# A two-layer hybrid trunk on one core: three sigmoids as Exp, Ln, Exp on ScalarE, and HGRN2's level products with two heads in the two halves of the array

## The chip, the cores and the metric

The kernel runs on one core of one Trainium2 chip. The metric is the device time in microseconds (us) of that core. Before the change the median of 3 runs is 2185.41 us (2184.63 to 2187.1).

## The reference, cut to what matters

Two layers over 512 tokens of width 1024 (256 context tokens and 256 latent tokens). Each layer normalizes, projects to a wide vector, runs three token mixers side by side (mLSTM, HGRN2, differential attention), projects back, and ends in a feed-forward block: a dense SwiGLU in layer 0, eight experts in layer 1. Everything is float32. The change touches HGRN2 and three gates:

```python
q = to_heads(jax.nn.silu(p['hg_q']), HG_H)            # silu(x) = x * sigmoid(x)
G = jnp.cumsum(g, axis=3)
a = jnp.einsum('bhntk,bhntsk,bhnsk->bhnts', q, decay, k)   # decay = exp(G_t - G_s), s <= t
o = jnp.einsum('bhnts,bhnse->bhnte', a, v) + ...           # both directions are added
jax.nn.sigmoid(p['ml_o']) * head_rms_norm(mlstm)           # 4 heads of 64
head_rms_norm(hgrn2) * jax.nn.silu(p['hg_g'])              # 4 heads of 64
```

HGRN2 has 4 heads with keys and values of width 64, so two heads fill the 128 partitions.

## The kernel before, in words

One function builds the program; a framework places each engine's instructions by its own estimate of when they are ready, so an instruction can stand ahead of one that was written earlier. Only stretches marked strict keep the written order, and none of the edits lies in one.

Products of float32 are made in two ways. Weights are split into a high part `whi` (ScalarE) and a low part `wlo` (VectorE), and three matmuls of the float32r type take the place of one (`mm3`). In HGRN2's levels the operands are plain float32, and the trace shows two weight loads and two matmuls for each product.

`mixer(l, X)` is one layer's mixer. `fm` is a generator that loads a megabyte of projection weights, multiplies 8 blocks for each 128 output columns into a bank `pp`, and hands the bank to a `use` function; `tm` does the same with tokens on the partitions. Generators wait in the list `work`, and `tick(n)` takes n steps out of it wherever the token mixers call it, so projection matmuls fill TensorE between the mixers' own. When `work` is empty, `tick` does nothing.

`use_hgq` (L752) turns the projected HGRN2 queries into silu: Exp on ScalarE, add 1 (L756) and reciprocal (L757) on VectorE, then the product. `use_o` (L993) does the same for the output gates of mLSTM and HGRN2, for four blocks of 128 columns a layer, each 128x512 in layer 0 and 128x256 in layer 1 (L998, L999). It is called late in the mixer, among the heads of the attention: `scores` and `values`, with softmax on ScalarE and VectorE. When the last `fm` is drained, `mix_t` transposes the mixers' output and multiplies it with the gates `og`.

`hgrn()` (L803) computes HGRN2 as a tree over token distance: distances 256 and 128 first (tiles `ez`), then for each pair of token tiles p0 seven levels with half widths h = 64, 32, 16, 8, 4, 2, 1, in a group of four and a group of three. Layer 0 has two pairs (14 levels), layer 1 one (7 levels). At the start of a group TensorE sums the logarithms of the gates into banks `pe` and ScalarE takes Exp into `el`. One level then is:

- VectorE, for each of two directions d: `el` times the keys in place (128x256), then the queries times `el` into a zero-padded tile `zq`. `zq` has room for two heads side by side; the head on partitions 0 to 63 fills its half of the columns, the other head the other half (L914 to L916: two instructions on 64 partitions), and the rest stays zero, set once by a memset on POOL (L801).
- TensorE: 8 products with all 128 rows and 128 moving columns, both heads in one product, because each head's rows meet zeros in the other head's columns. They go into two banks `pa`, one for each token tile i.
- `take` merges each bank into the result `at`: at the first level a copy on ScalarE, later a masked copy on VectorE (L890, 128x512), one for each token tile, so the first can start when half of the level's matmuls are done.
- then `tick(T_LEV)`: 4 steps of projections in layer 0, 3 in layer 1, as long as `work` lasts.

The diagonal after the last level (products `pa<-hq,hk`, masked copies at L938) already uses 64 rows for each head, and so do the products of `ez`.

Of the kernel before, what the change touches and what calls it, by code (L numbers as in the profile page):

```python
# [12 lines left out]
F32 = mybir.dt.float32  # L13
# [4 lines left out]
AF = mybir.ActivationFunctionType  # L18
ALU = mybir.AluOpType
AX = mybir.AxisListType  # L20

P = 128
# [87 lines left out]
def kernel(ctx: ExitStack, tc: tile.TileContext, t: dict, out: bass.AP):  # L110
    nc = tc.nc
# [3 lines left out]
    def ordered(op):  # L115
        def call(*args, **kw):
            ins = op(*args, **kw)  # L117
            if strict[0]:
                tc.keep_in_program_order(ins)
            return ins  # L120
        return call

    MM, TR = ordered(nc.tensor.matmul), ordered(nc.tensor.transpose)
    ACT = ordered(nc.scalar.activation)
    TT, TS = ordered(nc.vector.tensor_tensor), ordered(nc.vector.tensor_scalar)
# [12 lines left out]
    one = cp.tile([P, 1], F32, name="one")  # L138
# [10 lines left out]
    def bank(name, dt=F32):  # L149
        return psp.tile([P, 512], dt, tag="b", bufs=8, name=name)  # L150
# [374 lines left out]
    def mixer(l, X, banks=None):  # L525
# [16 lines left out]
        masks = mk.tile([P, 8, P], U8, name="masks")  # L542
# [16 lines left out]
        if l == 0:  # L559
            with tc.tile_pool(name=f"pn{l}", bufs=1) as pn:  # L560
# [56 lines left out]
                A, B, C = range(4), range(4, 6), range(6, 8)  # L617
# [30 lines left out]
        hg = hgp.enter_context(tc.tile_pool(name=f"hg{l}", bufs=1))  # L648
# [27 lines left out]
        def tm(ci, tiles, use):  # L676
# [3 lines left out]
            for n, g in enumerate(tiles):  # L680
# [11 lines left out]
                for i in g:  # L692
                    use(i, acc[i])


        hk = hx.tile([P, 2, 2, 512], F32, tag="b8a", name="hk")
        lh = hx.tile([P, 4, 4, P], F32R, tag="b8b", name="lh")
        ll = hx.tile([P, 4, 4, P], F32R, tag="b8c", name="ll")
        hq = hg.tile([P, 2, 512], F32, name="hq")
# [52 lines left out]
        def use_hgq(j, pp):  # L752
            e = hx.tile([P, 512], F32, tag="w2a", bufs=2, name="hq_e")
            a = slice(q0, 512)
            ACT(e[:, a], pp[:, a], AF.Exp, scale=-1.0)
            TS(e[:, a], e[:, a], scalar1=1.0, scalar2=None, op0=ALU.add)  # L756
            nc.vector.reciprocal(e[:, a], e[:, a])  # L757
            TT(hq[:, j, a], pp[:, a], e[:, a], op=ALU.mult)

        va = hg.tile([P, 4, 4, 65], F32, name="va")  # L760
# [35 lines left out]
                nc.vector.tensor_reduce(ss[:, 2 * n:2 * n + 2], sq, axis=AX.X, op=ALU.add)  # L796
            return ss

        zq = [hg.tile([P, 2, 2, P], F32, tag=f"zq{n}", name=f"zq{n}") for n in range(4)]
        for z0 in zq:  # L800
            nc.gpsimd.memset(z0, 0.0)  # L801

        def hgrn():  # L803
            opart = X[:, :, 256:512]
# [2 lines left out]
            for d in range(2):  # L807
                both = hx.tile([P, 2, 2, 512], F32, tag="w8", bufs=3, name=f"ez{d}")
                for li, lev in enumerate((256, 128)):
                    e = both[:, li]  # L810
# [20 lines left out]
                    for i0, i1 in (((0, 2), (2, 4)) if lev == 256 else tuple((i, i + 1) for i in range(lo // P, 4))):  # L831
                        key = i0 < 2 if lev == 256 else (i0 % 2 == 0) == (d == 0)
                        a = slice(i0 * P, i1 * P)
# [4 lines left out]
            half = [slice(0, 64), slice(64, 128)]  # L838
            for p0 in range(qt[0], 4, 2):
# [15 lines left out]
                if p0 == 2:  # L855
                    for s in range(2):
                        pa = [bank("pa") for _ in range(2)]
# [8 lines left out]
                pa = [bank("pa") for _ in range(2)]  # L866
# [8 lines left out]
                nc.vector.tensor_copy(opart[:, p0:p0 + 2, :], po.rearrange("p (i c) -> p i c", i=2))  # L875

            groups = (LEVELS[0:4], LEVELS[4:7])
            turn = 0  # L880
            for p0 in range(qt[0], 4, 2):
                pt_ = slice(p0 * P, p0 * P + 256)
                A = [hg.tile([P, 512], F32, tag="at", bufs=4, name="at") for _ in range(2)]

                def take(i, pa, n):
                    v = lambda a: a.rearrange("p (x t) -> p x t", x=4)
                    if n is None:
                        ACT(A[i], pa, AF.Copy)
                    else:
                        nc.vector.copy_predicated(v(A[i]), masks[:, n, :].unsqueeze(1).to_broadcast([P, 4, P]), v(pa))  # L890

                for gi, lv in enumerate(groups):
                    nl = len(lv)
                    z_ = []
                    for d in range(2):
                        e = hx.tile([P, 2, 4, 256], F32, tag="w8", bufs=3, name="el")
                        c0 = d * S_DIR + gi * 512
                        for c in range(2):
                            for i in range(2):
                                pe = bank("pe")  # L900
                                for part in (lh, ll):
                                    MM(pe[:, 0:nl * P], part[:, p0 + i, 2 * d + c, :], sums[:, c0:c0 + nl * P],
                                       start=(part is lh), stop=(part is ll))
                                ACT(e[:, c, 0:nl, i * P:(i + 1) * P], pe[:, 0:nl * P].rearrange("p (l t) -> p l t", l=nl), AF.Exp)
                        z_.append(e)
                    for n, h in enumerate(lv):
                        V = lambda a: a.rearrange("p c (n two h) -> p c n two h", two=2, h=h)
                        qs = []
                        for d in range(2):
                            ev = V(z_[d][:, :, n, :])  # L910
                            TT(ev[:, :, :, d, :], ev[:, :, :, d, :], V(hk[:, d, :, pt_])[:, :, :, d, :], op=ALU.mult)
                            q_ = zq[turn % len(zq)]
                            turn += 1
                            for par in range(2):  # L914
                                TT(q_[half[par], :, par, :].rearrange("p c (n h) -> p c n h", h=h), ev[half[par], :, :, 1 - d, :],
                                   V(hq[:, :, pt_])[half[par], :, :, 1 - d, :], op=ALU.mult)  # L916
                            qs.append(q_)
                        for i in range(2):
                            pa = bank("pa")
                            for c in range(2):  # L920
                                for d in range(2):
                                    MM(pa[:, c * 256:(c + 1) * 256].rearrange("p (a n two h) -> p a n two h", a=2, two=2, h=h)[:, :, :, 1 - d, :],
                                       z_[d][:, c, n, i * P:(i + 1) * P],
                                       qs[d][:, c, :, i * 64:(i + 1) * 64].rearrange("p a (n h) -> p a n h", h=h),
                                       start=True, stop=True, skip_group_check=True)
                            take(i, pa, None if gi + n == 0 else 4 * gi + n)
                        tick(T_LEV)
                pa = [bank("pa") for _ in range(2)]
                for i in range(2):
                    ia = slice((p0 + i) * P, (p0 + i + 1) * P)  # L930
                    for c in range(2):
                        for d in range(2):
                            for par in range(2):
                                at = i * 256 + c * P
                                MM(pa[par][:, at:at + P], hk[half[par], d, c, ia], hq[half[par], c, ia], start=(d == 0), stop=(d == 1))
                for par in range(2):
                    for i in range(2):
                        nc.vector.copy_predicated(A[i].rearrange("p (c a t) -> p c a t", c=2, a=2)[:, :, par, :],  # L938
                                                  masks[:, 7, :].unsqueeze(1).to_broadcast([P, 2, P]),
                                                  pa[par][:, i * 256:(i + 1) * 256].rearrange("p (c t) -> p c t", c=2))  # L940
                po = bank("po")
                for i in range(2):
                    for h in range(4):
                        MM(po[:, i * 256 + h * 64:i * 256 + (h + 1) * 64], A[i][:, h * P:(h + 1) * P], hv[:, p0 + i, h * 64:(h + 1) * 64],
                           start=(i + h == 0), stop=True, skip_group_check=True)
                o = opart[:, p0:p0 + 2, :]
                TT(o, po.rearrange("p (i c) -> p i c", i=2), o, op=ALU.add)
# [45 lines left out]
        def use_o(base):  # L993
            def use(j, pp):
                a = slice(q0, 512)
                o = og[:, base + j, a]
                ACT(o, pp[:, a], AF.Exp, scale=-1.0)
                TS(o, o, scalar1=1.0, scalar2=None, op0=ALU.add)  # L998
                nc.vector.reciprocal(o, o)  # L999
                w = vl + (V_MN, V_HN)[base // 2] + j  # L1000
                if base == 0:
                    TS(o, o, scalar1=sv[:, w:w + 1], scalar2=None, op0=ALU.mult)
                else:
                    STT(o, o, sv[:, w:w + 1], pp[:, a], op0=ALU.mult, op1=ALU.mult)
            return use
# [76 lines left out]
        for h in range(4):  # L1082
            if h % 2 == 0:

                S = [hx.tile([P, 4, 512], F32, tag=tg, name="S") for tg in ("b8b", "b8c")]
                for s in range(4):
                    a, b = st_rng[s]
# [8 lines left out]
            for d in range(2):  # L1096
# [10 lines left out]
                for s in range(4):  # L1107
                    W = hx.tile([P, 512], F32, tag="w2a", bufs=2, name="W")
                    bias = bT[:, s, row:row + 1]
# [14 lines left out]
                    for a, b in rng:  # L1124
                        for tt in range(a // P, b // P):
                            MM(num[d][:, tt, :], W[:, tt * P:(tt + 1) * P], va[:, s, h, :],
                               start=not started[d], stop=False, skip_group_check=True)
                            started[d] = True
            tr = slice(qt[0], 4)
            for d in range(2):  # L1130
# [7 lines left out]
                dst = hs_[:, tr, h * 64:(h + 1) * 64]  # L1138
# [47 lines left out]
        op = ow.enter_context(tc.tile_pool(name=f"ow{l}", bufs=1))  # L1186
# [120 lines left out]
        qs = {qt[0]: queries(qt[0])}  # L1307
        heads = [(tt, h) for tt in qt for h in range(4)]
        GATED = 8 if need else 6
        for n in range(len(heads) + 7):  # L1310
            if n < len(heads):
                tt, h = heads[n]
# [29 lines left out]
        with tc.tile_pool(name=f"xw{l}", bufs=1) as xw, tc.tile_pool(name=f"xo{l}", bufs=1) as xo:  # L1342
# [27 lines left out]
            two, three = steps  # L1370
# [591 lines left out]
```

## Time and profile before

| what | value |
| --- | --- |
| median of 3 runs | 2185.41 us |
| the profiled execution's own time | 2181.0 us |
| its span from first to last instruction | 2179.2 us |
| instructions in it | 27390 |
| mean granted TensorE clock | 0.985 of 2.4 GHz |
| PE / PEld busy | 2085.3 / 1672.8 us |
| VectorE (DVE) / ScalarE (ACT) busy | 1644.6 / 1249.3 us |
| POOL busy | 35.3 us |

PE is TensorE's matmul, PEld its weight load, which overlaps PE. The profile also gives windows (busy time of each engine in a stretch, the granted clock and the DMA share), the timeline (instructions in order of time, runs of equal ones merged: start, duration, engine, line, operation, how often, and in brackets the idle time before it with what ended it) and lists by tile. A helper issues most instructions, so most carry its line, L117, and are told apart by their tiles. In a merged row of n weight loads the last one starts one load's duration, 0.19 us, ahead of the row's end, so the distance between two starts is (duration - 0.19) / (n - 1).

### The profile page before, as it was taken

How to read it: one execution, taken by the hardware profiler on the slowest of the kernel's cores; microseconds unless marked ns; L12 is line 12 of the kernel's file. 1: busy time of each engine (PE TensorE's matmuls, PEld its weight loads, DVE VectorE, ACT ScalarE, POOL GpSimd, SP SyncE). 2: the span in 40 equal slices, each digit the busy share in tenths (PEclk: the TensorE clock that was granted, in tenths of full speed). 3: DMA queues.
4: the chain of work that ended last, by engine and by line, in shares of the span. 5: the costliest groups of instructions: out<-in, count | busy, mean ns of one | idle time of the engine just before them, and what ended most of it. 6: DMA issues, size and time to landing. Idle time of an engine off the chain costs nothing.

```text
span 2179.2 us, 27390 instructions
## 1 busy us (share of the span) xinstructions
PE 2085.3 (96%) x10326; PEld 1672.8 (77%) x10326; DVE 1644.6 (75%) x2324; ACT 1249.3 (57%) x1837; POOL 35.3 (2%) x47
## 2 busy tenths in 40 slices
PE   7998998999999999999879999999999999999997
PEld 4877776788788788887668888777778777777775
DVE  4758459769872347665879998888888888798987
ACT  3632455651222336534668776767777676767765
POOL 1000000010000001000000000000000000000000
PEclk9999999999999999999999999999999999999999
DMA  7430522238791331311258998899998999899992
GB/s 293 151 117 30 88 102 73 89 133 286 288 325 20 135 108 51 128 49 49 78 200 347 370 361 330 329 353 356 348 349 322 357 356 346 320 354 359 345 358 87
DMA packets 84301, 497.86 MB, mean 228 GB/s; under 512 B 19904, under 2 KB 20928, under 8 KB 26560
## 3 DMA queue, kind: packets, MB, share of 16 engines
q1 hardware_dynamic: 84160, 496.03, 61.8%
q8 instruction: 83, 1.36, 0.3%
q14 instruction: 58, 0.48, 0.1%
HBM read 493.86 MB, written 2.14 MB: 228 GB/s over the span
## 4 chain that ended last, share of the span: by engine, by line
PE 73%; DVE 16%; DMA 4%; ACT 4%; issue 3%; POOL 0%; SPq 0%; DVEq 0%; ACTq 0%; POOLq 0%
PE pg L117 20%; PE py L117 12%; PE pgu L117 10%; DVE wlo L117 9%; PE pp L117 8%; PE pd L117 5%; PE pr L117 4%; DMA raw<-w_eu 3%; PE st L117 3%; PE pa L117 2%; ACT whi L117 2%; PE po L117 1%; PE num L117 1%; PE pm L117 1%; DVE zq L117 1%
## 5 line engine op out<-in xcount | busy, mean ns | idle before, releaser
L117 DVE TENSOR_TENSOR wlo<-raw,whi 128x1024 fp32r<-128x1024 f32 x819 | 961.0, 1221 | 152.7 <-ACT whi L117 142.8
L117 ACT ACTIVATE whi<-raw 128x1024 fp32r<-128x1024 f32 (+1 forms) x820 | 813.2, 1055 | 187.3 <-PE pgu L117 75.6
L117 PE MATMUL pg<-wlo,TH 128*128 128x512 f32 x896 | 363.6, 406 | 5.8 <-DVE wlo L117 2.0
L117 PE MATMUL pg<-whi,TH 128*128 128x512 f32 x896 | 355.4, 397 | 0.0
L117 PE MATMUL pg<-whi,TL 128*128 128x512 f32 x896 | 352.1, 393 | 0.0
L117 PE MATMUL py<-whi,hhl 128*128 128x512 f32 x896 | 289.2, 394 | 0.0
L117 PEld LDWEIGHTS pg<-wlo,TH 128*128 128x128 f32 x896 | 168.3, 188 | 64.7 <-DVE wlo L117 31.3
L117 PEld LDWEIGHTS py<-whi,hhl 128*128 128x128 f32 x896 | 168.3, 188 | 39.4
L117 PEld LDWEIGHTS pg<-whi,TH 128*128 128x128 f32 x896 | 168.3, 188 | 39.3
L117 PEld LDWEIGHTS pg<-whi,TL 128*128 128x128 f32 x896 | 168.5, 188 | 35.1
L117 PE MATMUL py<-wlo,hhl 128*128 128x512 f32 x448 | 177.6, 396 | 1.0 <-DVE wlo L117 0.8
L117 ACT ACTIVATE hhl<-ph 128x512 fp32r<-128x512 f32 x56 | 33.4, 596 | 174.0 <-PE ph L1728 174.0
L117 PE MATMUL pgu<-TH,whi 128*128 128x512 f32 x320 | 127.2, 398 | 2.7 <-ACT whi L117 2.7
L117 PE MATMUL pgu<-TH,wlo 128*128 128x512 f32 x320 | 127.3, 398 | 0.2 <-DVE wlo L117 0.2
L117 PE MATMUL pgu<-TL,whi 128*128 128x512 f32 x320 | 127.0, 397 | 0.0
L117 PE MATMUL pp<-TH,whi 128*128 128x512 f32 (+1 forms) x304 | 117.9, 388 | 0.0
L117 PE MATMUL pp<-TH,wlo 128*128 128x512 f32 (+1 forms) x304 | 110.8, 365 | 0.4 <-DVE wlo L117 0.4
L117 PE MATMUL pp<-TL,whi 128*128 128x512 f32 (+1 forms) x304 | 111.1, 366 | 0.0
L274 DVE CUSTOM_DVE_ANT_0 junk<-raw,srow,sv 128x1024 bf16<-128x1024 f32 x80 | 102.5, 1282 | 3.4 <-DMA srow<-gd 2.0
L117 PEld LDWEIGHTS py<-wlo,hhl 128*128 128x128 f32 x448 | 84.1, 188 | 21.6 <-DVE wlo L117 2.7
L117 DVE TENSOR_TENSOR hhl<-ph,hhl 128x512 fp32r<-128x512 f32 x56 | 38.6, 690 | 55.4 <-ACT hhl L117 55.3
L117 PEld LDWEIGHTS pgu<-TH,whi 128*128 128x128 f32 x320 | 60.5, 189 | 17.6 <-ACT whi L117 3.2
(341 smaller groups left out, 3146.7 us busy)
## 6 DMA issues: line engine op xcount, KB each, us to landing
raw<-w_eg SPq DMA_DIRECT2D x112, 1024.0 KB, 6.3
raw<-w_eu SPq DMA_DIRECT2D x111, 1024.0 KB, 6.2
raw<-w_ed SPq DMA_DIRECT2D x111, 1024.0 KB, 6.5
raw<-w_mv SPq DMA_DIRECT2D x28, 1024.0 KB, 7.3
raw<-w_fm SPq DMA_DIRECT2D x22, 1024.0 KB, 4.9
raw<-w_fg SPq DMA_DIRECT2D x11, 1024.0 KB, 7.0
raw<-w_fu SPq DMA_DIRECT2D x11, 1024.0 KB, 5.4
raw<-w_fd SPq DMA_DIRECT2D x11, 1024.0 KB, 5.0
```

Of the source, the lines that this page charges most:

```text
L117: ins = op(*args, **kw)
L274: nc.vector.tensor_tensor_reduce(junk, w[:, j * 1024:(j + 1) * 1024], srow[:, s, :], 1.0, sv[:, b:b + 1], ALU.mult, ALU.add, modT[l][:, f, ...
```

## The change

A helper `sigmoid` computes 1/(1+exp(-x)) as exp(-ln(1+exp(-x))), all three steps on ScalarE; `use_hgq` and `use_o` call it. The zero padding and its memsets go. `zq` holds both heads on their own partitions, 128x256, written by one instruction for each direction. A level has 16 products of 64 rows and 64 moving columns, in pairs on the upper and lower rows of the array; the head on partitions 0 to 63 goes to one bank, the other head to a second. `take` merges a level with four copies of 128x256 and follows the level's last product.

```diff
+        def sigmoid(dst, src):
+            ACT(dst, src, AF.Exp, scale=-1.0)
+            ACT(dst, dst, AF.Ln, bias=one)
+            ACT(dst, dst, AF.Exp, scale=-1.0)
...
-            ACT(e[:, a], pp[:, a], AF.Exp, scale=-1.0)
-            TS(e[:, a], e[:, a], scalar1=1.0, scalar2=None, op0=ALU.add)
-            nc.vector.reciprocal(e[:, a], e[:, a])
+            sigmoid(e[:, a], pp[:, a])
...
-        zq = [hg.tile([P, 2, 2, P], F32, tag=f"zq{n}", name=f"zq{n}") for n in range(4)]
-        for z0 in zq:
-            nc.gpsimd.memset(z0, 0.0)
+        zq = [hg.tile([P, 512], F32, tag=f"zq{n}", name=f"zq{n}")[:, 0:256].rearrange("p (c t) -> p c t", c=2) for n in range(4)]
...
-                def take(i, pa, n):
-                    v = lambda a: a.rearrange("p (x t) -> p x t", x=4)
-                    if n is None:
-                        ACT(A[i], pa, AF.Copy)
-                    else:
-                        nc.vector.copy_predicated(v(A[i]), masks[:, n, :].unsqueeze(1).to_broadcast([P, 4, P]), v(pa))
+                def take(pa, n):
+                    for par in range(2):
+                        for i in range(2):
+                            a = A[i].rearrange("p (c a t) -> p c a t", c=2, a=2)[:, :, par, :]
+                            b = pa[par][:, i * 256:(i + 1) * 256].rearrange("p (c t) -> p c t", c=2)
+                            if n is None:
+                                ACT(a, b, AF.Copy)
+                            else:
+                                nc.vector.copy_predicated(a, masks[:, n, :].unsqueeze(1).to_broadcast([P, 2, P]), b)
...
-                            for par in range(2):
-                                TT(q_[half[par], :, par, :].rearrange("p c (n h) -> p c n h", h=h), ev[half[par], :, :, 1 - d, :],
-                                   V(hq[:, :, pt_])[half[par], :, :, 1 - d, :], op=ALU.mult)
+                            TT(q_.rearrange("p c (n h) -> p c n h", h=h), ev[:, :, :, 1 - d, :],
+                               V(hq[:, :, pt_])[:, :, :, 1 - d, :], op=ALU.mult)
...
+                        pa = [bank("pa") for _ in range(2)]
                         for i in range(2):
-                            pa = bank("pa")
                             for c in range(2):
                                 for d in range(2):
-                                    MM(pa[:, c * 256:(c + 1) * 256].rearrange("p (a n two h) -> p a n two h", a=2, two=2, h=h)[:, :, :, 1 - d, :],
-                                       z_[d][:, c, n, i * P:(i + 1) * P],
-                                       qs[d][:, c, :, i * 64:(i + 1) * 64].rearrange("p a (n h) -> p a n h", h=h),
-                                       start=True, stop=True, skip_group_check=True)
-                            take(i, pa, None if gi + n == 0 else 4 * gi + n)
+                                    for par in range(2):
+                                        at = i * 256 + c * P
+                                        MM(pa[par][:, at:at + P].rearrange("p (n two h) -> p n two h", two=2, h=h)[:, :, 1 - d, :],
+                                           z_[d][half[par], c, n, i * P:(i + 1) * P],
+                                           qs[d][half[par], c, i * 64:(i + 1) * 64].rearrange("p (n h) -> p n h", h=h),
+                                           start=True, stop=True, skip_group_check=True)
+                        take(pa, None if gi + n == 0 else 4 * gi + n)
...
-                ACT(o, pp[:, a], AF.Exp, scale=-1.0)
-                TS(o, o, scalar1=1.0, scalar2=None, op0=ALU.add)
-                nc.vector.reciprocal(o, o)
+                sigmoid(o, pp[:, a])
```

## Rows read from the trace of the kernel before

**Rows 1.** The profile's page: busy time by engine, and the chain that ended last.

```profile
PE 2085.3 (96%) x10326; PEld 1672.8 (77%) x10326; DVE 1644.6 (75%) x2324; ACT 1249.3 (57%) x1837; POOL 35.3 (2%) x47
PE 73%; DVE 16%; DMA 4%; ACT 4%; issue 3%; POOL 0%; SPq 0%; DVEq 0%; ACTq 0%; POOLq 0%
```

**Rows 2.** Windows: stretch, length, busy PE PEld DVE ACT POOL, PEclk, DMA share, GB/s.

```profile
75.00:100.00 25.00, 25.00 (x123) 20.66 (x122) 22.05 (x29) 16.64 (x29) 0.00 (x0) 1.00 0.25 87
148.00:168.00 20.00, 19.58 (x127) 15.66 (x127) 15.16 (x32) 6.05 (x12) 0.00 (x0) 1.00 0.25 78
168.00:183.00 15.00, 11.57 (x97) 10.30 (x95) 13.09 (x28) 4.11 (x9) 0.00 (x0) 1.00 0.18 73
183.00:215.00 32.00, 25.83 (x193) 22.71 (x193) 26.92 (x62) 9.12 (x19) 0.00 (x0) 1.00 0.00 1
...
860.00:880.00 20.00, 20.00 (x138) 18.31 (x138) 17.81 (x36) 19.16 (x32) 4.20 (x6) 1.00 0.34 101
...
932.00:951.00 19.00, 18.59 (x122) 16.20 (x121) 14.67 (x31) 8.15 (x14) 0.00 (x0) 1.00 0.17 56
951.00:967.00 16.00, 13.07 (x99) 11.70 (x97) 13.26 (x29) 3.17 (x8) 0.00 (x0) 0.89 0.01 1
```

**Rows 3.** Timeline of VectorE within the levels of layer 0's second pair.

```profile
196.30 0.42 DVE L117 TENSOR_TENSOR el<-el,hk 128x256 f32<-128x256 f32 x1
...
196.64 0.84 DVE L117 TENSOR_TENSOR zq<-el,hq 64x256 f32<-64x256 f32 x2
197.51 1.35 DVE L890 COPY_PREDICATED at<-masks,pa 128x512 f32<-128x512 uint8 x2
...
198.76 0.41 DVE L117 TENSOR_TENSOR el<-el,hk 128x256 f32<-128x256 f32 x1
...
214.45 1.44 DVE L938 COPY_PREDICATED at<-masks,pa 128x256 f32<-128x256 uint8 x4 [0.37 <-PE pa L117]
```

**Rows 4.** Timeline of PEld, layer 0: 128-row, 64-row, then 128-row products; a level's 16.

```profile
141.38 1.99 PEld L117 LDWEIGHTS po<-hv,ab 128*128 128x128 f32 x16
141.61 1.89 PE L117 MATMUL po<-hv,ab 128*128 128x64 f32 x16
143.43 0.97 PEld L117 LDWEIGHTS pa<-ez 64*128 64x128 f32 x16
...
144.53 0.19 PEld L117 LDWEIGHTS pp<-TH,whi 128*128 128x128 f32 x1
...
157.42 1.98 PEld L117 LDWEIGHTS pa<-zq,el 128*128 128x128 f32 x16
```

**Rows 5.** The tiles og and hf_e: operations, duration ns min/median/max, first and last start.

```profile
L117 DVE TENSOR_SCALAR og<-og x8: 284/350/427, 348.1 to 1091.0; 128x512 f32<-128x512 f32 x4, 128x256 f32<-128x256 f32 x4
L999 DVE RECIPROCAL og<-og x8: 1733/2539/3348, 349.5 to 1092.5; 128x512 f32<-128x512 f32 x4, 128x256 f32<-128x256 f32 x4
...
L117 ACT ACTIVATE hf_e<-hf_e x16: 613/626/636, 64.2 to 884.9; 128x512 f32<-128x512 f32 x16
L117 ACT ACTIVATE hf_e<-hf_e,one x16: 705/714/724, 65.3 to 885.6; 128x512 f32<-128x512 f32 x16
```

**Rows 6.** Windows of the attention with the output gates, layer 0 and layer 1.

```profile
375.00:380.00 5.00, 2.05 (x8) 0.97 (x7) 4.97 (x11) 0.30 (x2) 0.00 (x0) 1.00 0.00 0
380.00:385.00 5.00, 2.30 (x11) 2.30 (x12) 4.96 (x10) 2.25 (x6) 0.00 (x0) 0.54 0.00 0
385.00:390.00 5.00, 4.20 (x16) 2.60 (x16) 5.00 (x10) 2.85 (x7) 0.00 (x0) 0.78 0.55 210
...
1100.00:1105.00 5.00, 1.00 (x4) 1.00 (x5) 5.00 (x17) 2.99 (x10) 0.00 (x0) 0.90 0.01 4
1105.00:1110.00 5.00, 4.31 (x28) 3.82 (x28) 1.94 (x4) 2.10 (x5) 0.00 (x0) 0.75 0.40 120
```

**Rows 7.** Layer 1's levels, timeline and window: a level at the lower clock.

```profile
956.38 2.71 PEld L117 LDWEIGHTS pa<-zq,el 128*128 128x128 f32 x16 [1.37 <-issue]
...
958.00:959.00 1.00, 1.00 (x7) 1.00 (x6) 0.52 (x2) 0.00 (x0) 0.00 (x0) 0.50 0.00 0
```

## The prediction

> **What bounds the kernel now.** I read the page first: TensorE is busy for 96% of the span and holds 73% of the chain that ended last, VectorE 16% [rows 1]. So an edit is worth what it gives back of the time in which TensorE waits or runs slowly, and work taken off VectorE is worth nothing where TensorE is full. That is read stage by stage, from the windows. Three kinds of stage touch the change.
>
> First, the levels while `work` still holds projections: four levels of layer 0's first pair and four of layer 1. TensorE is busy 19.58 of 20 us and 18.59 of 19 [rows 2]. I call these 8 levels filled; TensorE is their limit.
>
> Second, the levels after `work` has run out: 3 of layer 0's first pair, 7 of its second, 3 of layer 1, so 13 unfilled levels. TensorE is busy 11.57 of 15, 25.83 of 32 and 13.07 of 16 us and idles for 3.4 + 6.2 + 2.9 = 12.5 us; VectorE is busy 13.09, 26.92 and 13.26 us [rows 2]. Here VectorE is the limit, together with the handing over between the two.
>
> Third, the attention with the output gates. VectorE is full (4.97, 4.96 and 5.00 of 5 us) while TensorE is busy 2.05, 2.30 and 4.20 of 5 in layer 0 and 1.00 of 5 in layer 1, and after each gap the granted clock is down (0.54, 0.78, 0.75, between the levels 1.2 and 2.4 GHz) [rows 6].
>
> The stage of the query sigmoids is none of these: TensorE is busy 25.00 of 25 us in layer 0 and 20.00 of 20 in layer 1 [rows 2].
>
> **The change, part by part.**
>
> *Query sigmoids.* Two blocks a layer lose an add and a reciprocal on VectorE and gain a Ln and an Exp on ScalarE, 0.71 + 0.63 us in the 128x512 form [rows 5]. Full TensorE hides both. The cover in layer 0 is ScalarE's slack, 16.64 of 25 us busy. In layer 1 ScalarE is busy 19.16 of 20 [rows 2]; there the blocks are half as wide, and some 1.5 us of ScalarE could delay weight splits. I cost both at 0, with 0 to +1.5 for the range.
>
> *Levels, VectorE.* One direction now takes 0.34 us for `el` (196.30 to 196.64) and 0.87 for two `zq` (to 197.51), the two masked copies 1.25 (to 198.76) [rows 3]. A level is 2 x (0.34 + 0.87) + 1.25 = 3.67 us. After: one `zq` of 128x256 per direction, between 0.34 (the `el` product has the same shape) and 0.43 (half the pair); I take 0.43, the same operands. Four copies of 128x256 have a row: 1.44 us [rows 3]. A level is 2 x (0.34 + 0.43) + 1.44 = 2.98, so 0.69 less, 9.0 us over 13 levels. Not all comes through. The copies now wait for the level's last product, where the first one used to start at half; at the end of each stretch nothing covers that. TensorE's own 25.83 us in the second pair leave at most 6.2 to gain. I take two thirds, **-6**; range -9 to 0. In the filled levels VectorE's gain is worth nothing.
>
> *Levels, TensorE.* 16 loads of a level start (1.98 - 0.19)/15 = 0.119 us apart, 1.91 a level. The 64-row products start (0.97 - 0.19)/15 = 0.052 apart, since two row halves run side by side; 32 of them take 1.66 [rows 4]. Those rows have 128 moving columns, the new products 64. I take the same distance, because 128-row products with 64 columns keep the distance of those with 128 (1.99 us for 16) [rows 4]: the weight load sets it. So -0.25 a level. Against that stands the change of rows. Into 64 rows: the last 128-row load starts at 143.18, the next at 143.43, 0.25 instead of 0.119; back: from 144.21 to 144.53, 0.32 instead of 0.052 [rows 4]. That is +0.40 for a filled level, which stands between projections. Net +0.15 x 8 = **+1.2**. The bounds: distance halved again, 32 x 0.026 = 0.83, gives -0.68 x 8 = -5.4; no overlap at all, 32 x 0.119 = 3.81, gives +2.30 x 8 = +18. I stay with 0.052, the only row with 64 rows.
>
> The Trainium skill (TensorEngine Tiling (Array Packing), Theoretical Speedup) promises up to 2x where the contraction is 64 or less. Read on these products it would bring a level to 0.95 us; the rows above speak against it, as 128 columns hide the load and 64 don't. By it the sum would be some 5 us lower; it is the fourth rival.
>
> *Rest of the levels.* The first level's copies are four narrower ones on ScalarE, which is busy 9.12 of 32 us [rows 2]: 0. The memsets went on an otherwise idle POOL: 0.
>
> *Output gates.* VectorE loses 4 x (3.35 + 0.43) = 15.1 us in layer 0 and 4 x (1.73 + 0.28) = 8.0 in layer 1; ScalarE gains 4 x (0.71 + 0.63) = 5.4 and about half of that [rows 5]. What can come back is what TensorE lost. Layer 0, 375 to 390: idle 2.95 + 2.70 + 0.80 = 6.45 us. A clock of 0.54 means 0.92 of that stretch at half speed; 2.30 us busy would shrink by 1.1, and 0.78 gives another 0.9. Together 8.5 [rows 6]. Layer 1: idle 4.0 + 0.7, and half of 1105 to 1110 at half speed gives 1.1, together 5.8 [rows 6]. VectorE stops being full, but softmax still goes from VectorE to ScalarE to TensorE and back, so a part of the gaps stays; ScalarE is busy 0.30 to 2.99 of 5 there and has room. I take three quarters, -6.4 and -4.4, **-10.8**; range -14 to -3.
>
> *Sum.* -6 + 1.2 - 10.8 = -15.6. From the profiled execution's 2181.0 us that is 2165.4. That execution lies 4.4 us under the median of the runs, 2185.4; on the median the sum gives 2169.8. The stages that follow keep their own lengths, since their loads start when buffers come free and move along.
>
> **Rivals.**
>
> 1. *Slower: VectorE waits out each level.* A level's four copies become ready together, after its 16th product. If the built order puts them ahead of the next level's `el` and `zq`, products and VectorE take turns: 1.54 + 1.66 + about 0.1 + 1.44 = 4.74 us a level instead of 3.67, +13.9 over 13 levels instead of -6; with +1.2 and -10.8 that is +4.3, and with 0.40 for rows switched once more in the stretches about +5: 2190. It decides from about 4.4 us a level on. Against it: now a level's `el` runs among the copies of the one before (copies at 197.51, `el` at 196.30 and 198.76 [rows 3]). 0.07.
>
> 2. *The clock falls in the unfilled levels.* TensorE's work there shrinks in columns, and in layer 1 the clock already fell to 1.2 GHz amid these levels, where 16 loads took 2.71 us instead of 1.98 [rows 2, 4, 7]. In layer 0 it held at 1.00 with TensorE busy 25.83 of 32 us [rows 2]. At half clock a level's products take 2 x 1.66 = 3.3 us, more than VectorE's 2.98, and the `pe` sums double too: instead of -6 I get about +2 to +4, so -6 to -8 in all, near 2179, or 2183 with the matmuls behind each stretch starting slow. 0.12, half of it within 0.2%.
>
> 3. *The gates' gain stays hidden.* If softmax's chain, not VectorE's load, opens the gaps, the gates give -3 and the sum is -8: 2178. Against it: VectorE is full in every window with a gap [rows 6]. 0.08.
>
> 4. *The level's products halve on TensorE.* Filled levels then gain 5.4 instead of losing 1.2: 2163. 0.06. The Trainium skill's page named above states the factor this needs.
>
> **How the numbers follow.** The forecast has 0.67, and its time is 2170 us. Its own range is -23 (both VectorE terms at their bounds) to -7: 2162 to 2178. The range over all cases reaches to rivals 2, 3 and 4, 2160 to 2183; only rival 1 and the tails lie outside. No change means within 0.2%, 4.4 us, about what a measurement of this kernel can tell. Faster: 0.67 + 0.08 + 0.06 and half of rival 2, less a little for a weak outcome of both main terms, 0.81. Same: 0.12. Slower: rival 1, 0.07.
>
> **What would show it.** In the trace after: no reciprocal at the gates; VectorE no longer full at 375 to 390 and its gap on TensorE gone, with the clock at 1.00 there; 4 to 6 us less from the first `el` to the last copy of layer 0's second pair, levels about 3.0 to 3.3 us apart; 32 loads of a level in about 1.7 us, with 0.25 to 0.3 us at each change of rows; filled levels not shorter. I am wrong if the 64-column products stand 0.1 us apart, if the copies stand ahead of the next level's `el`, if the clock is under 1.00 in 168 to 215, or if the gaps at the gates stay although VectorE has room.

## The result, and the profile after

The changed kernel takes 2171.14 us (median of 4 runs, 2169.21 to 2177.84) beside 2185.02 for the kernel before: ratio 0.9941, interval 0.9918 to 0.9964. Its profiled execution is the longest of the four, 2177.84 us with a span of 2176.1. One execution of the kernel before, in the second group of runs below, took 7142.31 us beside 2174.3 to 2187.33 for the other fifteen; its ratios leave it out. The page's busy times and chain:

```profile
PE 2096.1 (96%) x10662; PEld 1684.6 (77%) x10662; DVE 1596.4 (73%) x2294; ACT 1261.1 (58%) x1867; POOL 30.3 (1%) x39
PE 70%; DVE 16%; DMA 5%; ACT 4%; issue 4%; POOL 0%; SPq 0%; DVEq 0%; ACTq 0%; POOLq 0%
```

VectorE lost 48 us of work and TensorE gained 11 [rows 1], with 336 more matmuls. These are windows of the stages that were changed: layer 0's levels (148 to 226), its attention with the gates (375 to 390) and layer 1's levels without projections (947 to 964). Columns as in [rows 2].

```profile
148.00:168.00 20.00, 20.00 (x188) 15.39 (x188) 10.44 (x28) 5.83 (x13) 0.00 (x0) 1.00 0.25 80
168.00:188.00 20.00, 16.78 (x147) 15.74 (x147) 12.22 (x33) 4.11 (x9) 0.00 (x0) 0.66 0.14 54
188.00:216.00 28.00, 25.84 (x250) 23.47 (x250) 17.33 (x49) 9.35 (x21) 0.00 (x0) 0.80 0.01 1
216.00:226.00 10.00, 8.95 (x83) 8.31 (x82) 4.47 (x13) 0.63 (x1) 0.00 (x0) 0.86 0.00 1
375.00:380.00 5.00, 5.00 (x30) 3.89 (x29) 4.83 (x17) 4.78 (x14) 0.00 (x0) 1.00 0.09 34
380.00:385.00 5.00, 4.85 (x30) 3.21 (x27) 5.00 (x11) 2.81 (x8) 0.00 (x0) 1.00 0.00 0
385.00:390.00 5.00, 4.12 (x18) 2.64 (x18) 5.00 (x13) 4.05 (x10) 0.00 (x0) 1.00 0.00 0
947.00:964.00 17.00, 14.99 (x154) 14.26 (x152) 10.89 (x32) 3.17 (x8) 0.00 (x0) 0.80 0.01 1
```

Two things are to be seen. At layer 0's gates the gap on TensorE is all but gone (it idles 1.03 of 15 us instead of 6.45) and the clock is full, against 2.05 and 2.30 busy and a clock of 0.54 in [rows 6]. In layer 0's levels that find no projections the clock fell to 0.66 and 0.80, where [rows 2] had 1.00; in layer 1, where it had fallen before too (0.89 over 16 us [rows 2]), it is 0.80 over 17 us. The next two fences are from the changed kernel's timeline, TensorE and then VectorE, in those levels:

```profile
172.71 4.72 PE L117 MATMUL pa<-zq,el 64*128 64x64 f32 x56 [0.56 <-DVE zq L117]
179.31 0.69 PE L117 MATMUL pa<-zq,el 64*128 64x64 f32 x4 [1.87 <-DVE zq L117]
...
180.29 2.87 PE L117 MATMUL pa<-zq,el 64*128 64x64 f32 x25
...
182.96 0.42 PE L117 MATMUL pa<-zq,el 64*128 64x64 f32 x1
...
192.29 0.63 PE L117 MATMUL pe<-sums,lh 128*128 128x512 f32 x1
...
195.33 0.39 PE L117 MATMUL pe<-sums,lh 128*128 128x512 f32 x1
195.56 0.39 PE L117 MATMUL pe<-sums,ll 128*128 128x512 f32 x1
```

```profile
177.41 1.43 DVE L894 COPY_PREDICATED at<-masks,pa 128x256 f32<-128x256 uint8 x4 [1.36 <-PE pa L117]
178.74 0.76 DVE L117 TENSOR_TENSOR zq<-el,hq 128x256 f32<-128x256 f32 x2
183.41 1.43 DVE L894 COPY_PREDICATED at<-masks,pa 128x256 f32<-128x256 uint8 x4 [3.91 <-PE pa L117]
```

From 180.29 on the products stand (2.87 - 0.42)/24 = 0.102 us apart, and the sums behind them take 0.63 us each until the clock is back and they take 0.39. VectorE, the limit of these levels before, now waits 1.36 and 3.91 us for TensorE. In windows of 2 us the moment of the fall can be seen:

```profile
172.00:174.00 2.00, 1.44 (x27) 1.33 (x25) 2.00 (x6) 0.56 (x1) 0.00 (x0) 1.00 0.00 0
174.00:176.00 2.00, 2.00 (x28) 2.00 (x25) 2.00 (x5) 0.00 (x0) 0.00 (x0) 0.60 0.00 0
176.00:178.00 2.00, 1.43 (x14) 1.24 (x12) 0.64 (x3) 0.00 (x0) 0.00 (x0) 0.50 0.00 0
...
194.00:196.00 2.00, 2.00 (x8) 1.62 (x7) 1.14 (x4) 1.48 (x3) 0.00 (x0) 0.78 0.00 0
```

The clock goes from 2.4 to 1.2 GHz within 174 to 176, while TensorE is busy without a break on a row of level products (in the 2 us before it was busy for 1.44), and comes back at 194 to 196, in the sums of the next group.

A balance of the two profiled executions, by marks that all kernels share (each a first or last start of a tile's operation), in us:

| stage | before | after |
| --- | --- | --- |
| levels of layer 0, from the first `el` to the first state copy | 78.5 | 85.5 |
| on to the first exponential of the attention | 111.5 | 113.0 |
| from there, over the gates, to the feed-forward's first product | 142.4 | 131.9 |
| the feed-forward's first products (`pgu`) | 228.1 | 224.8 |
| layer 1 from its last query silu to its last state copy | 137.8 | 138.8 |
| from there over its gates to the first expert | 162.5 | 162.9 |
| the experts | 983.0 | 983.0 |

With -0.4 ahead of the first `el` and +0.4 behind `pgu` that is -3.9 us up to the experts' last mark, and with +0.8 behind it the -3.1 of the two spans. The other three executions of the changed kernel were 7 to 9 us shorter and have no profile.

### The profile page after: what moved, and what is told of

The parts are those of the page before. It is cut to its first block, busy times and chain, and to the rows that moved or that the text cites. A ratio compares the mean times of both kernels' runs of the same rounds, so it can differ in the third digit from the quotient of the medians.

```text
span 2176.1 us, 28051 instructions
## 1 busy us (share of the span) xinstructions
PE 2096.1 (96%) x10662; PEld 1684.6 (77%) x10662; DVE 1596.4 (73%) x2294; ACT 1261.1 (58%) x1867; POOL 30.3 (1%) x39
## 4 chain that ended last, share of the span: by engine, by line
PE 70%; DVE 16%; DMA 5%; ACT 4%; issue 4%; POOL 0%; SPq 0%; DVEq 0%; ACTq 0%; POOLq 0%
PE pg L117 18%; PE py L117 12%; DVE wlo L117 10%; PE pp L117 8%; PE pgu L117 7%; PE pd L117 5%; PE pr L117 4%; PE pa L117 3%; DMA raw<-w_eu 3%; PE st L117 3%; ACT whi L117 2%; PE po L117 2%; PE num L117 1%; DMA raw<-w_ed 1%; PE pe L117 1%
```

## The experiments

**Repeat, and each half of the change alone.** Four kernels on one chip, beside a kernel before of 2182.81 us. The first is the changed kernel again.

> The changed kernel once more, unaltered, for a second profile and more times. In its first profile the granted clock fell to 1.2 GHz in the unfilled levels and that execution (2177.84 us) was the longest of four. Theory A (the clock there is a matter of the single execution): about 2171 us, and a profile near 2170 shows the clock at 1.00 in more of layer 0's levels. Theory B (the narrower products always let it fall): the same clocks of 0.5 to 0.8 in the levels of both layers whatever the time of the execution.

Measured: 2177.59 us, 0.9977 (0.9963 to 0.9991). Faster again, but by less; the two intervals just meet. Its profile shows the fall again, a clock of 0.74 in 168 to 188 us and 0.76 in 188 to 216, as its theory B had it. The mean granted clock that each execution reports goes with its time: in the first comparison three executions at 0.982 took 2169.21 to 2171.14 us and one at 0.978 took 2177.84; here nine of twelve lie under 0.980. Starts scatter as well: the first query silu, ahead of which nothing was changed, starts at 82.1 to 85.7 us over the profiled executions of all kernels here. So single figures below are read to about 3 us, and stages against stages.

`sig_only` is the kernel before with the three-step sigmoids:

```diff
-            ACT(e[:, a], pp[:, a], AF.Exp, scale=-1.0)
-            TS(e[:, a], e[:, a], scalar1=1.0, scalar2=None, op0=ALU.add)
-            nc.vector.reciprocal(e[:, a], e[:, a])
+            sigmoid(e[:, a], pp[:, a])
...
+                sigmoid(o, pp[:, a])
```

> The kernel before with both sigmoids on ScalarE and the levels as they were. Prediction's terms: gates -10.8, query sigmoids 0, so about 2174 us; TensorE's gap at 375 to 390 gone. If the levels bring nothing because the clock falls (rival 2), the sigmoids bring all of the measured -14: about 2171 us. If the gates' gain stays hidden (rival 3): -3, 2182 us.

Measured: 2171.08 us, 0.9953 (0.9936 to 0.997), by the ratio some 10 us under the kernel before. The stage over layer 0's gates is 132.4 us instead of 142.4; the other stages of the balance stay within 1 us of before. `levels_only` is the kernel before with the rest of the change (`zq`, products, `take`).

> The kernel before with the levels changed and the sigmoids as they were. Prediction's terms: -6 + 1.2, about 2180 us. Rival 2 (the clock falls in the unfilled levels): between 2184 and 2192 us, with the granted clock at 0.5 in 174 to 194 as in the changed kernel's first profile, where layer 0's levels ended 6.6 us later than before.

Measured: 2191.64 us, 1.0028 (1.001 to 1.0047): slower. Layer 0's levels take 88.4 us instead of 78.5, layer 1's stage 143.8 instead of 137.8. (The changed kernel had 138.8 there; in `levels_only` the clock is 0.50 from 971 to 983 us, longer than in the changed kernel, and why is not known.) Windows of the levels in `sig_only`, and then in `levels_only`:

```profile
168.00:188.00 20.00, 16.04 (x122) 13.61 (x120) 16.22 (x36) 6.70 (x14) 0.00 (x0) 1.00 0.04 15
188.00:216.00 28.00, 22.37 (x177) 20.24 (x178) 24.20 (x55) 4.99 (x11) 0.00 (x0) 1.00 0.01 2
```

```profile
168.00:188.00 20.00, 16.77 (x148) 15.68 (x147) 11.32 (x31) 3.92 (x9) 0.00 (x0) 0.66 0.09 33
188.00:216.00 28.00, 26.11 (x227) 24.17 (x227) 16.50 (x45) 9.36 (x21) 0.00 (x0) 0.72 0.01 1
```

With the old products the clock stays at 1.00 in layer 0 although TensorE idles 9.6 of 48 us; with the new ones it falls, and VectorE has room it can't use. All executions on this chip point the same way: their granted clock is 0.984 on average in both `sig_only` and the kernel before, 0.979 in the changed kernel and 0.976 in `levels_only`. So the sigmoids bring the gain, and the levels take part of it back. Both halves together would be 0.9953 + 0.0028 = 0.998, which is what the repeat shows. `spread` is the changed kernel with projections handed out in thinner portions, so that they last over more levels:

```diff
-STEPS = {"out": (3, 3), "lev": (4, 3), "scan": (8, 5), "ml": (8, 9), "da": (2, 2)}
+STEPS = {"out": (2, 2), "lev": (2, 3), "scan": (8, 5), "ml": (8, 9), "da": (2, 2)}
```

> The changed kernel with the projection steps handed out more thinly, 2 instead of 3 behind each block of the distances 256 and 128 and 2 instead of 4 behind each of layer 0's levels (2 and 3 in layer 1), so that they last through nearly all levels. If the fallen clock in the unfilled levels is what holds the change back, the clock stays at 1.00 there and the time is 5 to 12 us under the changed kernel's, about 2160 to 2166 us. If the clock costs nothing on the path, or the thinner filling opens as many gaps ahead of the levels, 2168 to 2174 us.

Measured: 2167.41 us, 0.9937 (0.9918 to 0.9955), the fastest of the four. Its windows:

```profile
168.00:188.00 20.00, 20.00 (x200) 16.46 (x197) 13.00 (x34) 6.20 (x12) 0.00 (x0) 1.00 0.15 53
188.00:216.00 28.00, 24.66 (x255) 21.16 (x252) 16.39 (x44) 6.03 (x14) 0.00 (x0) 0.82 0.16 58
```

Levels with projections beside them keep the full clock (1.00 in 168 to 188), the ones left over don't. From the first query silu to layer 0's first state copy it takes 145.7 us, against 151.2 in the changed kernel and 144.3 in `sig_only`: it wins back most of what that stage had lost, and no more.

**Is it the clock, or the exchange between the engines?** Four more on one chip, beside a kernel before of 2184.5 us. `filler` gives TensorE products that nothing reads, in the levels that find `work` empty:

```diff
+                        if not work:
+                            pf = bank("pe")
+                            for m in range(4):
+                                MM(pf, lh[:, p0, m, :], sums[:, 0:512], start=True, stop=True, skip_group_check=True)
```

> The changed kernel with four extra 128-row, 512-column matmuls behind every level at which no projections are left; their bank is read by nobody, so the computation is unchanged. They cost TensorE about 0.9 us a level, some 12 us over the 13 unfilled levels. Theory A (the fallen clock costs the levels their gain): the clock stands at 1.00 in 168 to 216, layer 0 from its first el to the first copy of S takes 77 to 82 us instead of 85.5 in the changed kernel and 78.5 before, and the time is 3 to 9 us under the changed kernel's. Rival W (the levels lose by the merges that wait for a level's last product and by the changes of rows, not by the clock): the extra matmuls come on top, 3 to 10 us over the changed kernel.

Measured: 2178.01 us, 0.9973 (0.9964 to 0.9983), as the changed kernel in its repeat. Its windows, and from its timeline a row of the same 56 products as at 172.71 above:

```profile
168.00:188.00 20.00, 18.87 (x198) 16.12 (x196) 12.48 (x33) 4.71 (x10) 0.00 (x0) 1.00 0.15 58
188.00:216.00 28.00, 27.76 (x273) 22.60 (x272) 18.10 (x50) 8.43 (x20) 0.00 (x0) 1.00 0.00 1
216.00:226.00 10.00, 9.57 (x88) 8.47 (x87) 5.51 (x17) 1.16 (x3) 0.00 (x0) 1.00 0.01 2
947.00:964.00 17.00, 16.84 (x179) 14.08 (x179) 10.06 (x28) 3.98 (x10) 0.00 (x0) 1.00 0.01 2
...
176.32 3.34 PE L117 MATMUL pa<-zq,el 64*128 64x64 f32 x56
...
183.69 0.27 PE L117 MATMUL pa<-zq,el 64*128 64x64 f32 x1
```

The clock holds at 1.00 throughout, and the 56 products take 3.34 us instead of 4.72, (3.34 - 0.27)/55 = 0.056 us apart. Layer 0's levels take 83.1 us, 2.4 less than after, though twelve rounds of four added matmuls stand in them on a nearly full TensorE (the lists by tile show 48 more `pe<-sums,lh` there than in the changed kernel); at 0.23 us each (195.33 to 195.56 above, sums of the same size at the full clock) that is 11 us. So without the fall and without the filler they would take some 72 us, and the fall costs up to some 13 us in layer 0: an estimate, not run. As a remedy it missed: the filler costs what the clock gives back.

`unpaired` is the changed kernel with the loop over the two heads outermost, so that a level's products use one half of the rows sixteen times and then the other:

```diff
-                        for i in range(2):
-                            for c in range(2):
-                                for d in range(2):
-                                    for par in range(2):
+                        for par in range(2):
+                            for i in range(2):
+                                for c in range(2):
+                                    for d in range(2):
```

> The changed kernel with the two heads' products one after the other in each level, all 8 of the upper rows, then all 8 of the lower, instead of in turns. If the halves of the array work side by side only when they take turns, a level's 32 loads start 0.11 us apart instead of 0.054 and take 3.5 to 3.8 us: 8 filled levels lose about 1.7 us each and the unfilled ones become TensorE's, 15 to 30 us over the changed kernel. If the turns don't matter: the same time as the changed kernel, or 2 us less since a first bank is done at half.

Measured: 2236.86 us, 1.0249 (1.0233 to 1.0265), with 119.4 us for layer 0's levels: by the ratios some 59 us over the changed kernel's repeat, where 15 to 30 were expected. The clock is lower too, 0.73 and 0.68 in 168 to 216 us, and how much of the loss is its share was not taken apart. Timeline of the weight loads of one level, in the changed kernel and then in `unpaired`, both at a clock of 1.00:

```profile
156.61 0.19 PEld L117 LDWEIGHTS pp<-TH,wlo 128*128 128x128 f32 x1
157.16 1.86 PEld L117 LDWEIGHTS pa<-zq,el 64*128 64x128 f32 x32 [0.36 <-issue]
159.09 0.19 PEld L117 LDWEIGHTS pp<-TH,whi 128*128 128x128 f32 x1
```

```profile
164.60 3.25 PEld L117 LDWEIGHTS pa<-zq,el 64*128 64x128 f32 x32 [0.37 <-issue]
```

(1.86 - 0.19)/31 = 0.054 us from load to load against (3.25 - 0.19)/31 = 0.099. Here the two halves of the array gave that factor only in pairs that alternate.

`rows_only` has the new products and copies, but the queries padded with zeros as before, written by two instructions for each direction:

```diff
+                            for par in range(2):
+                                TT(q_[half[par], :, par, :].rearrange("p c (n h) -> p c n h", h=h), ev[half[par], :, :, 1 - d, :],
+                                   V(hq[:, :, pt_])[half[par], :, :, 1 - d, :], op=ALU.mult)
...
-                                           qs[d][half[par], c, i * 64:(i + 1) * 64].rearrange("p (n h) -> p n h", h=h),
+                                           qs[d][half[par], c, par, i * 64:(i + 1) * 64].rearrange("p (n h) -> p n h", h=h),
```

> The changed kernel with VectorE's part of a level as before, two 64-partition instructions for each direction into the padded tile, and the new 64-row products. Theory A': the 64-row products let the clock fall, whatever VectorE's pace: clocks of 0.5 to 0.8 in 174 to 216 as in the changed kernel, and 0 to 6 us over it. Rival: it is VectorE's shorter part and its new order that hand TensorE longer gaps: then the clock stands at 1.00 as before the change and the time is within 3 us of the kernel with the sigmoids alone.

Measured: 2197.67 us, 1.0067 (1.0052 to 1.0082). Its windows:

```profile
168.00:188.00 20.00, 17.44 (x140) 16.68 (x139) 13.46 (x35) 4.11 (x9) 0.00 (x0) 0.62 0.12 48
188.00:216.00 28.00, 25.25 (x177) 22.15 (x175) 16.45 (x43) 8.13 (x17) 0.00 (x0) 0.68 0.00 1
```

The clock falls with the 64-row products whether VectorE is quick or not, and here no gain of VectorE stands against it: layer 0's levels take 99.5 us. By the ratios that is some 20 us over the changed kernel's repeat, where 0 to 6 were expected; what makes it so much was not taken apart. `sig_spread` is `sig_only` with the thin portions of `spread`.

> The kernel with the sigmoids alone (levels as before) and the projection steps handed out more thinly, as in the run spread. If thinner filling pays by itself, 2 to 6 us under the kernel with the sigmoids alone. If it pays only because it keeps the clock up for the 64-row products, 0 to 4 us over the kernel with the sigmoids alone, since the clock never fell there. The version with the lowest time of the four combinations is the one to keep.

Measured: 2171.95 us, 0.9952 (0.994 to 0.9964), as `sig_only`. The old levels gain nothing that can be seen from more cover.

**Can the clock be held more cheaply?** Three kernels, beside a kernel before of 2184.36 us. `filler2` has `range(2)` in place of `filler`'s `range(4)`.

> The kernel after, with half of the filler: 2 instead of 4 extra matmuls of 128 rows and 512 columns (0.46 us at the full clock) behind each level that finds no projections left, 6 us in all 13. Theory A (the fall of the clock is what the levels lose, and the four matmuls only cost more than needed): the granted clock stays at 1.00 in 148 to 226 us, layer 0's levels take some 78 to 80 us from the first el to the first S copy instead of 83.1 (filler) and 85 (after), and the time is 3 to 6 us under filler's, 2172 to 2175. Theory B (with less filler the clock falls as in the kernel after): 0.66 to 0.80 in 168 to 216 us, 85 us or more for the levels, and the time is after's, 2178, or up to 6 us over it. Theory C (the clock holds, but the exchange between VectorE and TensorE sets the levels): clock 1.00, levels still near 83 us, time equal to filler's.

Measured: 2174.33 us, 0.9962 (0.9944 to 0.998); layer 0's levels 81.9 us. Windows:

```profile
168.00:188.00 20.00, 17.46 (x161) 14.97 (x160) 10.97 (x29) 3.79 (x8) 0.00 (x0) 0.83 0.01 5
188.00:216.00 28.00, 27.18 (x305) 23.05 (x305) 20.28 (x57) 8.43 (x20) 0.00 (x0) 1.00 0.01 1
```

Half the filler still holds the clock in the second pair, not in the first, and the levels are the shortest of the new kind. In the time it can't be told from `filler`. The second pair, which has no projections, shows what the new levels take at the full clock. From the first pair's diagonal copies to the second pair's, on VectorE's timeline before and then in `filler2`:

```profile
182.58 1.44 DVE L938 COPY_PREDICATED at<-masks,pa 128x256 f32<-128x256 uint8 x4 [0.29 <-PE pa L117]
...
214.45 1.44 DVE L938 COPY_PREDICATED at<-masks,pa 128x256 f32<-128x256 uint8 x4 [0.37 <-PE pa L117]
```

```profile
185.10 1.44 DVE L947 COPY_PREDICATED at<-masks,pa 128x256 f32<-128x256 uint8 x4 [2.79 <-PE pa L117]
...
215.02 1.43 DVE L947 COPY_PREDICATED at<-masks,pa 128x256 f32<-128x256 uint8 x4
```

That is 31.87 us before (and in `sig_only`) and 29.92 in `filler2`, with 14 added matmuls and the clock at 1.00; the same stretch takes 33.43 in `filler`, with 28 added, and 34.61 in the changed kernel, with none and a clock of 0.80. So at the full clock the new levels are quicker than the old even with the filler. Without its 3.2 us they would take 26.7, about 5 less than before: an estimate, and what the prediction had for this pair (4 to 6 less). `spread_fill2` puts the same two matmuls into `spread`.

> spread with the two extra matmuls of 128 rows and 512 columns behind each level that finds no projections left. In spread layer 0 still runs at 0.82 of the full clock in 188 to 216 us, some levels without projections. Theory A (the clock is what is left to win): clock 1.00 in 188 to 216 us, and 2 to 5 us under spread, about 2163 to 2165 beside a kernel before of 2183. Theory B (spread has left too few slow levels for it): the matmuls cost 2 to 4 us and give as much back, within 0.1% of spread.

Measured: 2174.89 us, 0.9953 (0.9935 to 0.997), with the clock at 0.89 in 188 to 216 us and 85.4 us for the levels: the filler gained nothing there, and neither expectation was met. Beside it `spread` once more:

> spread once more, beside the two kernels with two filler matmuls, on the same chip. If spread's first comparison stands: 0.9937 of the kernel before, within 0.9918 to 0.9955, some 2167 to 2171 for a before of 2183. If it was as much a matter of the chip as the first comparison of the kernel after (0.9941, then 0.9977): 0.995 to 0.997.

Measured: 2168.31 us, 0.993 (0.9908 to 0.9952). So the best version here is `spread`, 0.6 to 0.7% under the kernel before in both comparisons. From `spread_fill2`, 0.2% slower beside it, and from `sig_only`, which keeps the old levels, its intervals don't part it.

## Why the prediction was right or wrong

The time was right, in both comparisons within the range, but partly by luck: one of the sum's two large terms came out with the wrong sign, and the other with the wrong split. Point by point:

- **Query sigmoids, 0**: right. From the first query silu to the first `el` it is 65.7 us before, after and in `sig_only`.
- **Output gates, -10.8**: right in sum, wrong in its split. Layer 0 gave -10.5 (-10.0 in `sig_only`) where -6.4 was forecast, three quarters of the 8.5 that the windows showed as lost: over the whole stage TensorE idles 6.2 us less and is busy 4.3 us less, with a clock of 1.00 instead of 0.98. VectorE still is full at 375 to 390 with softmax, against the forecast that it would not be, but TensorE is no longer kept waiting. Its adds and reciprocals are gone, and the two steps that ScalarE gained take 0.73 + 0.64 us at most, as the tile `og` shows:

```profile
L117 ACT ACTIVATE og<-pp x8: 378/482/602, 355.5 to 1086.1; 128x512 f32<-128x512 f32 x4, 128x256 f32<-128x256 f32 x4
L117 ACT ACTIVATE og<-og,one x8: 498/622/726, 356.2 to 1086.6; 128x512 f32<-128x512 f32 x4, 128x256 f32<-128x256 f32 x4
L117 ACT ACTIVATE og<-og x8: 407/535/642, 356.9 to 1088.3; 128x512 f32<-128x512 f32 x4, 128x256 f32<-128x256 f32 x4
```

  Layer 1 gave 0 where -4.4 was forecast: there the third rival holds. The product that waits, in the timeline before and then in the changed kernel's, and windows of the latter:

```profile
1104.00 2.07 PE L117 MATMUL po<-dv,pT 128*128 128x128 f32 x8 [4.15 <-ACT pT L117]
...
1098.24 2.08 PE L117 MATMUL po<-dv,pT 128*128 128x128 f32 x8 [4.32 <-ACT pT L117]
...
1093.90:1098.20 4.30, 0.02 (x1) 0.00 (x0) 4.21 (x16) 3.35 (x11) 0.00 (x0) 0.75 0.21 76
1095.90:1100.90 5.00, 2.66 (x12) 2.53 (x12) 2.99 (x11) 2.65 (x8) 0.00 (x0) 0.51 0.00 0
1100.90:1105.90 5.00, 4.31 (x20) 3.95 (x19) 0.00 (x0) 1.79 (x4) 0.00 (x0) 0.50 0.00 0
```

  TensorE waits 4.32 us for `pT`, the transposed probabilities, where it waited 4.15 before. The removed reciprocals were not in this gap: the last one starts at 1092.5 [rows 5], and before the change the gap runs from 1099.85 to 1104.00. VectorE is as full in it as before, 4.21 of 4.30 us, with other work of the softmax and the gates. Layer 0's gap hung on another wait, on VectorE itself:

```profile
382.70 1.12 PE L1165 MATMUL pt<-ident,X 128*128 128x128 f32 x4 [4.63 <-DVE mf L117]
```

  So the trace before told the two layers apart, and the prediction, which argued from VectorE being full "in every window with a gap", took them for one. That reading was not right either: in the window from 1105 TensorE idles 0.69 us with VectorE busy 1.94 of 5 [rows 6]. Behind the gap layer 1 now runs at 0.51 and 0.50 for 10 us, where [rows 6] had 0.90 and 0.75. From the last state copy to the last gated tile (`mf`) it is 3.1 us shorter, and 3.7 longer from there to the last square of the mixer's output (`po_sq`).
- **Levels on VectorE, -6**: the step that failed. VectorE does each level in what was worked out, four copies in 1.43 and two `zq` in 0.76 us. But it is not the limit any more. In the place of that gain the clock fell, and TensorE became the limit: the second rival came true in the place it was given, though its price was too low: +2 to +4 instead of -6 was its term, and the levels of both layers, with the stretch behind layer 0's, cost 7.0 + 1.5 + 1.0 = +9.5. In `levels_only` the two level stages alone cost 9.9 + 6.0. Of the forecast's reasons against that rival, that [rows 2] held 1.00 with TensorE busy 25.83 of 32 us, the row was true and the conclusion wrong: those products had 128 rows and 128 columns. At the full clock the term would have held (26.7 us for 31.87 in the second pair, by `filler2`). The count of levels was off as well: `filler` has 68 added matmuls, so `work` is empty behind 17 levels, where 13 were counted.
- **Levels on TensorE, +1.2**: right in its distance, 0.054 us measured for 0.052, and at the change back to 128 rows, 158.83 to 159.09 us, 0.26 for 0.32. The change into 64 rows was dearer, 156.61 to 157.16, 0.55 for 0.25. The distance didn't halve again, so the fourth rival is out. (That 128 columns hide the load and 64 don't, as was argued against it, no row shows: 16 full-row loads take 1.98 us with 128 columns and 1.99 with 64 [rows 4].) The Trainium skill (TensorEngine Tiling (Array Packing), Theoretical Speedup) has up to 2x for such contractions; the trace comes near it in the distance of loads, 0.119 to 0.054, but a level has twice the loads, so its 16 and its 32 take 1.98 [rows 4] and 1.86 us.
- **First rival**: not what made the levels longer. In the changed kernel's timeline VectorE does `el` and `zq` of several levels in a row from 207.69 to 211.87, with no copy between. In places copies do stand ahead of a later `zq`, as at 177.41 and 178.74 above, where TensorE then waits 1.87 us. But in all of layer 0's levels its waits for `zq` fell from 9.2 to 4.3 us; what grew is its busy time, at a lower clock: 56.0 of 66 us before (150 to 216) and 66.6 of 73 after (150 to 223).
- **Later stages keep their lengths**: wrong by 3.3 us. The feed-forward's first products took 224.6 to 225.9 us in all kernels with the new levels but `filler` (227.2), and 227.9 to 228.2 in those with the old. One wait of `pgu` for `whi`, 2.7 us before and 0.7 after, makes most of it. What moves it was not tried, so its cause is open.

So the levels lost where they were to gain, and layer 0's gates and the feed-forward paid for it. That the first comparison landed within 1.2 us of the forecast's 2170 is partly its scatter, three of four executions at the higher clock of 0.982; the repeat's 2177.6, or -5 us by its ratio, is nearer to the second rival (-6 to -8, 2179).

## What to carry to other kernels

Time each part of a change alone: here one half gives 0.5% and the other takes 0.3% back, which the sum hides. Where no large products stand beside them, smaller products can cost the clock and so more time than they save, as here; look at the granted clock of that stretch, not at its busy time alone, and lay other large products over it, as `spread` does. A gap on TensorE beside a full VectorE may still hang on a chain of waits: relieving VectorE closed the gap in layer 0 and left it at 4.32 us in layer 1, and the releaser of the wait, in brackets in the timeline before, differed between the two.

## What was not expected of the hardware

- The clock fell from 2.4 to 1.2 GHz at 174 to 176 us while TensorE was shown busy 2.00 of 2 us with 64-row, 64-column float32 products; with 128-row, 128-column ones it stayed at 1.00 where TensorE idled 5.6 of 28 us (`sig_only`). In layer 1 it fell with those too (0.89 [rows 2]), and whether the rows, the columns or the two together make the difference in layer 0 was not tried.
- With two 512-column products behind each level the granted clock was 0.83 in 168 to 188 us and 1.00 in 188 to 216, with four 1.00 in both.
- 64-row loads stand 0.099 us apart on one half of the rows and 0.054 when the halves alternate.
